# Gate weights stored by 64 tokens in two halves, and 16 gathered rows moved to the last stage

## The chip, the core and the metric

The kernel runs on one core of one Trainium2 chip. The time is device microseconds from start to end of one execution; lower is better. The kernel before takes 2756.99 us, the median of three runs (2752.73 to 2758.27 us). Engines are named as the profile names them: PE is the matrix engine (TensorE) and PEld its weight loads, DVE is VectorE, ACT is ScalarE, POOL is GpSimd, SP is SyncE, which issues most of the DMAs.

## The reference

One transformer-like layer on 1024 tokens of width 1024. A norm and a projection feed a differential attention and a gated linear recurrence; both go through an output projection into the residual. Then comes the part that fills most of the time: for each token, 8 heads pick 16 of 16384 experts (two searches among 128 keys, then the best 16 of their sums), each expert is a single neuron with a row of `expert_down` and a row of `expert_up`, and the chosen 128 rows are weighted, summed and added to the residual. A last norm gives the output.

```python
def peer_ffn(xn, w_query, sub_keys_1, sub_keys_2, expert_down, expert_up):
    ...
    q = (xt @ w_query).reshape(T, PEER_HEADS, 2, PEER_HALF).astype(jnp.float32)
    s1 = jnp.einsum('thd,kd->thk', q[:, :, 0], sub_keys_1.astype(jnp.float32))
    s2 = jnp.einsum('thd,kd->thk', q[:, :, 1], sub_keys_2.astype(jnp.float32))
    v1, i1 = lax.top_k(s1, PEER_TOPK)
    v2, i2 = lax.top_k(s2, PEER_TOPK)
    cand = (v1[..., :, None] + v2[..., None, :]).reshape(T, PEER_HEADS, PEER_TOPK * PEER_TOPK)
    sc, ci = lax.top_k(cand, PEER_TOPK)
    eid = (jnp.take_along_axis(i1, ci // PEER_TOPK, axis=-1) * PEER_N_KEYS
           + jnp.take_along_axis(i2, ci % PEER_TOPK, axis=-1))
    g = jax.nn.softmax(sc, axis=-1)
    ...
        u = expert_down[eb]
        act = jax.nn.gelu(jnp.einsum('thkd,td->thk', u, xb).astype(jnp.float32))
        w = (gb * act).astype(xb.dtype)
        return jnp.einsum('thk,thkd->td', w, expert_up[eb])

def reference(x, ...):
    ...
        n = rmsnorm(h, norm1_g[l])
        p = n @ w_in[l]
        ...
        attn_out = diff_attention(q, k, v, lam, subln_g[l], lambda_init)
        lru_out = rglru_branch(xr, gate, ...)
        h = h + jnp.concatenate([attn_out, lru_out], axis=-1) @ w_out[l]
        h = h + peer_ffn(rmsnorm(h, norm2_g[l]), ...)
    return rmsnorm(h, norm_f_g)
```

## The kernel before

The 1024 tokens are eight blocks of 128. Three blocks (384 tokens, `NG`) do the expert part by *gathering*: for each of a block's 128 slots, POOL issues an indirect DMA that fetches one row of 1024 floats for each of the 128 tokens (line 879, 512 KB), and DVE uses it in one SCALAR_TENSOR_TENSOR, a dot product with the token for `expert_down` (line 896) or a scaled addition into `accg` for `expert_up` (line 906). That is 768 *gathered rows* in all, through five row buffers. Both kinds of DVE instruction are kept in program order.

The other five blocks (640 tokens, `TD`) do the expert part densely over all 16384 experts. An expert tile is the 128 experts that share the first key; there are 128 tiles. For each tile a *down* (`down_all`, 48 matmuls of 320 columns) gives `ga`, the activations of 128 experts by 640 tokens; its weights come by SP as `draw` (512 KB) and are split into a high part `dh` (ACT, line 126) and a low part `dl` (DVE, line 127), two pairs a down. The activations are multiplied by the *gate weights* (zero wherever an expert was not chosen, `ga<-ga,gw`), split into `w_h` and `w_l`, and 30 matmuls a tile (15 for each half of the columns, tile `pu`) add the products with `expert_up` (`uraw`, split into `uh` and `ul`).

The gate weights are made beforehand, in the *one-hot stage*: for 16 tokens at a time (`TB`, here a *block of 16*; there are 40), DVE builds one-hot rows `o` (line 1136) and weighted ones `o1v` (line 1140), ACT builds `o1a` (line 1147, 16 instructions), and 48 matmuls (line 1160) give for each token a 128 by 128 square of weights in PSUM tiles `pg` of four tokens. ACT copies each into a staging tile `st` (line 1163), laid out as [128 experts, 128 keys, `TG` tokens]. When a staging tile has its 32 tokens, two DMAs on ACT's queue (lines 1165 and 1166) store it to `gw_d`, the first 32 keys apart from the other 96. In the last stage SP loads the gate weights of four tiles at a time (`gw`, line 1198, 1280 KB), in runs of 4 keys by 32 tokens, 512 bytes.

Downs can run early: 70 of the 128 are done ahead of the last stage, during the queries, the top-k and above all beside the one-hots, so that PE has work there; their results are kept (`act`, written by ACT's queue). So in the one-hot stage PE alternates between 48 matmuls of a down and 48 of a block of 16.

Gathered rows are spread over the program by counts: `gather_steps(n)` puts n of them behind a piece of other work. `G_ATT`, `G_OUT`, `G_QRY`, `G_TOPK` and `G_OH` say how many fall into the second attention, the second output projection, the second queries, the top-k and the one-hots, and `G_UP` is what remains for the last stage, 466 of the 768. These counts are the program's order. The order on each engine is then made by a scheduler, which plays the program through with estimated times, and lets an instruction pass others on its engine where these are not ready; so where a gathered row stands on DVE is not given by the counts alone.

## Time and profile before

| | |
|---|---|
| median of three runs | 2756.99 us |
| the profiled execution | 2756.29 us, of which its span (first to last instruction) 2754.5 us |
| PE busy | 2626.9 us (95%) |
| DVE busy | 2276.4 us (83%) |
| ACT busy | 1200.6 us (44%) |
| HBM read and written | 690.77 MB and 102.11 MB |

The stages by time from the span's start: the projections and the two attentions to 568 us; the second output projection to about 660 us; the queries and the top-k, with the first early downs, to about 1020 us; the one-hots with early downs to 1408 us; the last stage to 2739 us; the final norms to the end. A busy PE can be short of its peak, since the ends of its matmuls are modelled; the starts of matmuls that follow each other tell its pace.

### The profile page before, as it was taken

The page shows a single profiled execution, that of the slowest core. Times are in us where ns is not written, and L with a number is a line of the kernel's source. Part 1 is how long each engine was busy: PE and PEld are TensorE (multiplying, and loading weights), DVE is VectorE, ACT ScalarE, POOL GpSimd, SP SyncE. Part 2 cuts the span into 40 slices and gives each one's busy share as a digit, 9 for nine tenths or more (in the row PEclk, how much of TensorE's full clock was granted, in tenths as well). Part 3 has the DMA queues.
Part 4 walks back from the last instruction along what each step waited for, and adds up shares of the span by engine and source line. Part 5 has one row for each costly group of instructions (what it writes and reads, how often), then busy time and mean ns, then how long its engine had stood idle before and what let it go on. Part 6 is the DMA issues. An engine that isn't in the chain of part 4 may idle for free.

```text
span 2754.5 us, 43406 instructions
## 1 busy us (share of the span) xinstructions
PE 2626.9 (95%) x15577; PEld 2323.2 (84%) x15577; DVE 2276.4 (83%) x4737; ACT 1200.6 (44%) x2551; POOL 1042.8 (38%) x850
## 2 busy tenths in 40 slices
PE   7989987889999899999999999999999999999996
PEld 6767965747999899999988888888888888888885
DVE  6565878877999978989967789888888888888897
ACT  5763436722324667888853223222223222222222
POOL 1000223353322015443323445444454545545563
PEclk9999988989999999999999999999999999999998
DMA  5446888877675249999999999999999999999986
GB/s 193 154 138 230 314 242 238 259 256 271 233 255 174 92 162 350 356 341 335 338 370 326 334 351 326 336 332 352 339 332 336 330 340 326 348 338 338 338 288 242
DMA packets 319273, 795.75 MB, mean 289 GB/s; under 512 B 26209, under 2 KB 126577, under 8 KB 316497
## 3 DMA queue, kind: packets, MB, share of 16 engines
q0 software_dynamic: 118128, 428.28, 44.2%
q1 hardware_dynamic: 184112, 297.97, 32.1%
q10 hardware_dynamic: 16816, 66.72, 6.0%
q8 instruction: 122, 2.00, 0.3%
q14 instruction: 95, 0.77, 0.1%
HBM read 690.77 MB, written 102.11 MB: 288 GB/s over the span
## 4 chain that ended last, share of the span: by engine, by line
PE 70%; issue 11%; DMA 9%; DVE 6%; POOL 2%; ACT 2%; SPq 0%; DVEq 0%; ACTq 0%; POOLq 0%
PE pu L158 9%; PE pu L161 9%; PE pu L162 9%; PE pd L162 8%; PE pd L158 8%; PE pd L161 8%; PE pg L1160 4%; PE pa L158 3%; PE pa L162 2%; PE pa L161 2%; POOL row L879 2%; DMA row<-in_expert_up,eid 2%; DMA row<-in_expert_down,eid 2%; DVE row L896 1%; PE pa L606 1%
## 5 line engine op out<-in xcount | busy, mean ns | idle before, releaser
L879 POOL DMA_INDIRECT row<-in_expert_up,eid x384 | 513.1, 1336 | 666.9 <-DVE accg L906 542.2
L879 POOL DMA_INDIRECT row<-in_expert_down,eid x384 | 487.9, 1271 | 631.0 <-DVE row L896 504.2
L158 PE MATMUL pd<-xdH,dh 128*128 128x320 f32 x2048 | 639.6, 313 | 6.0 <-ACT dh L126 3.8
L162 PE MATMUL pd<-xdH,dl 128*128 128x320 f32 x2048 | 631.3, 311 | 10.8 <-DVE dl L127 10.8
L161 PE MATMUL pd<-xdL,dh 128*128 128x320 f32 x2048 | 634.6, 310 | 0.0
L906 DVE SCALAR_TENSOR_TENSOR accg<-row,wg,accg 128x1024 f32<-128x1024 f32 x384 | 491.3, 1279 | 27.0 <-DMA row<-in_expert_up,eid 24.1
L161 PE MATMUL pu<-ul,w_h 128*128 128x512 f32 x1280 | 503.5, 393 | 2.5 <-DVE ul L127 2.5
L162 PE MATMUL pu<-uh,w_l 128*128 128x512 f32 x1280 | 499.6, 392 | 0.0
L896 DVE SCALAR_TENSOR_TENSOR row<-row,x2g 128x1024 f32<-128x1024 f32 x384 | 460.6, 1218 | 32.3 <-DMA row<-in_expert_down,eid 29.9
L162 PEld LDWEIGHTS pd<-xdH,dl 128*128 128x128 f32 x2048 | 385.4, 189 | 19.4 <-DVE dl L127 12.8
L158 PE MATMUL pu<-uh,w_h 128*128 128x512 f32 x1280 | 393.5, 394 | 8.3 <-DVE acc L1261 3.3
L158 PEld LDWEIGHTS pd<-xdH,dh 128*128 128x128 f32 x2048 | 387.0, 189 | 14.5 <-ACT dh L126 4.1
L161 PEld LDWEIGHTS pd<-xdL,dh 128*128 128x128 f32 x2048 | 386.8, 189 | 8.2
L126 ACT CAST uh<-uraw 128x512 fp32r<-128x512 f32 x256 | 157.9, 620 | 498.3 <-PE pu L162 397.5
L161 PEld LDWEIGHTS pu<-ul,w_h 128*128 128x128 f32 x1280 | 241.9, 189 | 50.3 <-DVE ul L127 3.7
L158 PEld LDWEIGHTS pu<-uh,w_h 128*128 128x128 f32 x1280 | 238.1, 189 | 52.5 <-issue 3.7
L162 PEld LDWEIGHTS pu<-uh,w_l 128*128 128x128 f32 x1280 | 241.3, 189 | 47.8
L126 ACT CAST dh<-draw 128x512 fp32r<-128x512 f32 x256 | 157.9, 618 | 241.5 <-PE pd L161 226.9
L127 DVE TENSOR_TENSOR ul<-uraw,uh 128x512 fp32r<-128x512 f32 x256 | 175.5, 687 | 77.6 <-ACT uh L126 76.7
L127 DVE TENSOR_TENSOR dl<-draw,dh 128x512 fp32r<-128x512 f32 x256 | 175.4, 687 | 67.3 <-ACT dh L126 65.2
L126 ACT CAST w_h<-ga 128x640 fp32r<-128x640 f32 x128 | 93.3, 729 | 243.1 <-PE pu L161 166.3
L1147 ACT ACTIVATE o1a<-o,slot_a 128x128 bf16<-128x128 bf16 x640 | 194.1, 428 | 1.8 <-DVE o L1136 1.8
(282 smaller groups left out, 4050.7 us busy)
## 6 DMA issues: line engine op xcount, KB each, us to landing
draw<-in_down_t SPq DMA_DIRECT2D x128, 512.0 KB, 7.0
uraw<-in_up_h SPq DMA_DIRECT2D x128, 512.0 KB, 7.2
gw<-gw_d SPq DMA_DIRECT2D x32, 1280.0 KB, 15.2
gw_d<-st ACTq DMA_DIRECT2D x20, 1536.0 KB, 10.4
act<-ga ACTq DMA_DIRECT2D x70, 320.0 KB, 4.9
ga<-act SPq DMA_DIRECT2D x70, 320.0 KB, 9.7
w_d<-w POOLq DMA_DIRECT2D x32, 512.0 KB, 5.1
w<-w_d SPq DMA_DIRECT2D x32, 512.0 KB, 5.5
```

The source lines that it names most:

```text
L126: A.copy(hi, src)
L127: (eng or V).tensor_sub(lo, src, hi.bitcast(F32))
L158: t = T.matmul(ps, wh, mh, start=first, stop=False)
L161: T.matmul(ps, wh, ml, start=False, stop=False)
L162: T.matmul(ps, wl, mh, start=False, stop=last)
L606: T.matmul(pss[:, t - t0, :], qt[:, t * P:(t + 1) * P], kt[:, ct % 2, :], start=True, stop=True)
L879: nc.gpsimd.indirect_dma_start(out=r, out_offset=None, in_=table, in_offset=bass.IndirectOffsetOnAxis(ap=eids[tb][:, s:s + 1], axis=0))
L896: tc.keep_in_program_order(V.scalar_tensor_tensor(r, r, 1.0, x2, op0=ALU.mult, op1=ALU.mult, accum_out=act[:, s:s + 1]))
L906: tc.keep_in_program_order(V.scalar_tensor_tensor(acc, r, w[:, s:s + 1], acc, op0=ALU.mult, op1=ALU.add))
L1147: A.activation(oa[:, g, :, j], o[:, g, 1, :, j], AF.Copy, scale=slot_a[b][:, tt + t:tt + t + 1])
L1160: T.matmul(ps[:, t - t4, :], o[:, g, 0, :, j], part[:, g, :, j], start=i == 0, stop=i == 2)
```

## The change

Staging tiles hold 64 tokens in place of 32, and each is two tiles of 64 keys. So the copy out of PSUM becomes two copies of half the size (160 instructions become 320), 64 tokens are stored by three DMAs of 1, 1 and 2 MB in place of four of 0.5 and 1.5 MB, and a load of gate weights reads runs of 4 keys by 64 tokens, 1024 bytes, the same 1280 KB. There are three buffers of a half tile (16 KB a partition each) where there were two of a whole one of 32 tokens (16 KB). The one-hot tile `o21` gets two buffers in place of three. `G_OUT` goes from 24 to 8, and with it `G_UP` from 466 to 482.

```diff
--- before.py
+++ after.py
@@ -44,11 +44,11 @@
 EG = 8
 EQ = 4
 EARLY = 4
-TG = 32
+TG = 64
 TB = 16
 TI = 2
 
-G_ATT, G_OUT, G_QRY, G_TOPK, G_OH = 64, 24, 46, 0, 168
+G_ATT, G_OUT, G_QRY, G_TOPK, G_OH = 64, 8, 46, 0, 168
 G_UP = 2 * NG * SLOTS - (G_ATT + G_OUT + G_QRY + G_TOPK + G_OH)
 B_OUT, B_CHAIN, B_TURN, B_QRY, B_TOPK = 0, 3, 8, 8, 12
 A_STEPS, A_AHEAD, A_FILL, LRU_AT, WO_AT = 3, 4, 0.5, 0.7, 50
@@ -1113,7 +1113,7 @@
         v12_stack.close()
         tk_stack.close()
         oh = ph.enter_context(tc.tile_pool(name="oh", bufs=2))
-        st_pool = ph.enter_context(tc.tile_pool(name="stage", bufs=2))
+        st_pool = ph.enter_context(tc.tile_pool(name="stage", bufs=3))
         ps_g = ph.enter_context(tc.tile_pool(name="ps_g0", bufs=3, space=PSUM))
         key_f = oh.tile([P, P], F32, name="key_f", bufs=1)
         G.iota(key_f, pattern=[[1, P]], base=0, channel_multiplier=0,
@@ -1132,7 +1132,7 @@
                 return t[:, g0:g0 + GB, :, None, :].broadcast_to([P, GB, n, P, TI]).rearrange(
                     "p g n k i -> p (g n) k i")
 
-            o = oh.tile([P, GB, 2, P, TI], BF, name="o21", bufs=3)
+            o = oh.tile([P, GB, 2, P, TI], BF, name="o21", bufs=2)
             V.tensor_tensor(o.rearrange("p g n k i -> p (g n) k i"),
                             key_t[:, None, :, :].broadcast_to([P, GB * 2, P, TI]),
                             per_slot(slot_k[b], 2), op=ALU.is_equal)
@@ -1150,7 +1150,7 @@
 
         def weights(t0, o, parts):
             if t0 % TG == 0:
-                sts[t0 // TG] = st_pool.tile([P, NK, TG], F32, name="st")
+                sts[t0 // TG] = [st_pool.tile([P, NK // 2, TG], F32, name="st") for _ in range(2)]
             st = sts[t0 // TG]
             for t4 in range(0, TB, 4):
                 ps = ps_g.tile([P, 4, P], F32, name="pg")
@@ -1160,10 +1160,14 @@
                         T.matmul(ps[:, t - t4, :], o[:, g, 0, :, j], part[:, g, :, j],
                                  start=i == 0, stop=i == 2)
                 c = t0 % TG + t4
-                A.copy(st[:, :, c:c + 4], ps.rearrange("p t i -> p i t"))
+                for half in range(2):
+                    A.copy(st[half][:, :, c:c + 4],
+                           ps[:, :, half * NK // 2:(half + 1) * NK // 2].rearrange("p t i -> p i t"))
             if (t0 + TB) % TG == 0:
-                nc.scalar.dma_start(gw_d[0][t0 // TG], st[:, :E_FIRST, :])
-                nc.scalar.dma_start(gw_d[1][t0 // TG], st[:, E_FIRST:, :])
+                n = NK // 2 - E_FIRST
+                nc.scalar.dma_start(gw_d[0][t0 // TG], st[0][:, :E_FIRST, :])
+                nc.scalar.dma_start(gw_d[1][t0 // TG][:, :n, :], st[0][:, E_FIRST:, :])
+                nc.scalar.dma_start(gw_d[1][t0 // TG][:, n:, :], st[1])
 
         sts = {}
         last_five, last = last, None
```

The scheduler's order changes in more places than the diff. Counted on DVE, the gathered rows (lines 896 and 906) stand like this:

| stage, by DVE's own instructions | before | after |
|---|---|---|
| up to the second output projection | 61 | 61 |
| second output projection (lines 1000 to 1004) | 27 | 11 |
| from there to the first one-hot | 46 | 46 |
| first to last one-hot | 112 | 156 |
| from there to the first `ul` | 8 | 9 |
| last stage | 514 | 485 |

In the steady part of the one-hot stage, from the 60th to the 136th `dl` on DVE (38 downs), there stand 107 gathered rows (32 of line 896, 75 of line 906), 36 `o` and 35 `o1v` before, and 149 (53 and 96), 37 and 37 after. In the same stretch PE has 36 and 37 blocks of 16.

DVE in the middle of the one-hot stage before, two blocks of 16 (`o_13866` and `o_14024` are their one-hot tiles):

```order
L1136 TENSOR_TENSOR o_13866<-key_t,slot_k_8430 128x4096
L906 SCALAR_TENSOR_TENSOR accg<-row,wg,accg 128x1024
L127 TENSOR_TENSOR dl<-draw,dh 128x512 x2
L1140 TENSOR_TENSOR o1v<-o_13866,slot_w_8435 128x4096
L1136 TENSOR_TENSOR o_14024<-key_t,slot_k_8431 128x4096
L906 SCALAR_TENSOR_TENSOR accg<-row,wg,accg 128x1024 x2
L127 TENSOR_TENSOR dl<-draw,dh 128x512
L906 SCALAR_TENSOR_TENSOR accg<-row,wg,accg 128x1024
L127 TENSOR_TENSOR dl<-draw,dh 128x512
L906 SCALAR_TENSOR_TENSOR accg<-row,wg,accg 128x1024
L1140 TENSOR_TENSOR o1v<-o_14024,slot_w_8436 128x4096
```

and at the like place after, one block and the head of the next:

```order
L1136 TENSOR_TENSOR o_13900<-key_t,slot_k_8380 128x4096
L906 SCALAR_TENSOR_TENSOR accg<-row,wg,accg 128x1024
L1140 TENSOR_TENSOR o1v<-o_13900,slot_w_8385 128x4096
L906 SCALAR_TENSOR_TENSOR accg<-row,wg,accg 128x1024 x2
L127 TENSOR_TENSOR dl<-draw,dh 128x512
L906 SCALAR_TENSOR_TENSOR accg<-row,wg,accg 128x1024
L127 TENSOR_TENSOR dl<-draw,dh 128x512
L906 SCALAR_TENSOR_TENSOR accg<-row,wg,accg 128x1024
L1136 TENSOR_TENSOR o_14061<-key_t,slot_k_8381 128x4096
```

The piece of before has one gathered row in its first block and four in its second; the piece after has five in its one block. `o1v` also stands closer behind its own `o`.

DVE at the program's end, where `ul` is the last work that PE needs from DVE and `acc` takes the last sums from PE; before:

```order
L127 TENSOR_TENSOR ul<-uraw,uh 128x512
L906 SCALAR_TENSOR_TENSOR accg<-row,wg,accg 128x1024
L127 TENSOR_TENSOR ul<-uraw,uh 128x512
L906 SCALAR_TENSOR_TENSOR accg<-row,wg,accg 128x1024
L127 TENSOR_TENSOR ul<-uraw,uh 128x512
L906 SCALAR_TENSOR_TENSOR accg<-row,wg,accg 128x1024
L1261 TENSOR_TENSOR acc_16753<-acc_16753,pu 128x512
L906 SCALAR_TENSOR_TENSOR accg<-row,wg,accg 128x1024 x2
L1261 TENSOR_TENSOR acc_16754<-acc_16754,pu 128x512
L906 SCALAR_TENSOR_TENSOR accg<-row,wg,accg 128x1024
L1261 TENSOR_TENSOR acc_16755<-acc_16755,pu 128x512
```

and after, around the norm of the last gathered block (line 729), which follows its last row:

```order
L127 TENSOR_TENSOR ul<-uraw,uh 128x512
L142 SCALAR_TENSOR_TENSOR n_r<-n_t,n_r 128x1
L141 SCALAR_TENSOR_TENSOR n_t<-n_r,n_v 128x1
L142 SCALAR_TENSOR_TENSOR n_r<-n_t,n_r 128x1
L729 SCALAR_TENSOR_TENSOR row<-accg,n_r,gfb 128x1024
L127 TENSOR_TENSOR ul<-uraw,uh 128x512 x6
L1265 TENSOR_TENSOR acc_16853<-acc_16853,pu 128x512
L1265 TENSOR_TENSOR acc_16854<-acc_16854,pu 128x512
L1265 TENSOR_TENSOR acc_16855<-acc_16855,pu 128x512
L1265 TENSOR_TENSOR acc_16856<-acc_16856,pu 128x512
L1265 TENSOR_TENSOR acc_16857<-acc_16857,pu 128x512
L127 TENSOR_TENSOR ul<-uraw,uh 128x512 x7
```

The gathered rows ran to the last sums; now the last one stands ahead of the last 14 `ul`.

ACT where a staging tile is stored; before:

```order
L1165 DMA gw_d<-st 128x1024
L1166 DMA gw_d<-st 128x3072
L1147 ACTIVATE o1a<-o_12601,slot_a_8439 128x128 x5
L126 CAST dh<-draw 128x512
L1044 ACTIVATE ga<-pd 128x320
L126 CAST dh<-draw 128x512
L1044 ACTIVATE ga<-pd 128x320
L1163 COPY st<-pg 128x128x4
L1069 DMA act_12685<-ga 128x640
L1163 COPY st<-pg 128x128x4 x3
L1147 ACTIVATE o1a<-o_12759,slot_a_8440 128x128 x16
```

and after, where line 1164 is the half copy and the first three after the stores all go into the first half:

```order
L1168 DMA gw_d<-st 128x2048
L1169 DMA gw_d<-st 128x2048
L1170 DMA gw_d<-st 128x4096
L126 CAST dh<-draw 128x512
L1147 ACTIVATE o1a<-o_13576,slot_a_8390 128x128 x16
L1044 ACTIVATE ga<-pd 128x320
L126 CAST dh<-draw 128x512
L1044 ACTIVATE ga<-pd 128x320
L1164 COPY st<-pg 128x64x4 x3
L1069 DMA act_13660<-ga 128x640
L1164 COPY st<-pg 128x64x4 x5
```

Copies into the second half need the buffer that lines 1168 and 1169 have just begun to store; before, the tile that the next copies fill had been stored two blocks of 16 earlier.

## Rows read from the trace of the kernel before

**Rows 1.** The page: busy time, share and instructions of each engine.

```profile
PE 2626.9 (95%) x15577; PEld 2323.2 (84%) x15577; DVE 2276.4 (83%) x4737; ACT 1200.6 (44%) x2551; POOL 1042.8 (38%) x850
```

**Rows 2.** Stages: length, busy of PE, PEld, DVE, ACT, POOL; clock, DMA share, GB/s.

```profile
570.00:660.00 90.00, 86.04 (x291) 46.86 (x290) 72.96 (x146) 20.97 (x39) 46.52 (x37) 0.98 0.89 317
1076.00:1409.00 333.00, 333.00 (x3278) 329.31 (x3277) 300.32 (x261) 293.91 (x803) 140.29 (x95) 1.00 0.93 343
1409.00:1500.00 91.00, 81.97 (x465) 75.59 (x464) 61.48 (x96) 26.75 (x49) 28.86 (x24) 0.96 1.01 362
1500.00:2500.00 1000.00, 1000.00 (x5128) 876.72 (x5126) 839.66 (x1168) 280.72 (x488) 498.12 (x392) 1.00 0.95 335
2700.00:2755.00 55.00, 32.92 (x121) 25.51 (x120) 42.50 (x93) 12.22 (x29) 15.62 (x12) 0.81 0.61 216
```

**Rows 3.** Chain of waits, in order of time: two one-hot blocks.

```profile
1155.69 2.77 PE pg L1160 x48
...
1165.55 2.77 PE pg L1160 x48
```

**Rows 4.** Timeline of VectorE in one block: start, length, work, idle before it.

```profile
1158.43 2.29 DVE L1140 TENSOR_TENSOR o1v<-o,slot_w 128x4096 bf16<-128x4096 bf16 x1 [0.37 <-PE pg L1160]
1160.64 2.28 DVE L1136 TENSOR_TENSOR o<-key_t,slot_k 128x4096 bf16<-128x4096 bf16 x1
...
1163.99 1.22 DVE L896 SCALAR_TENSOR_TENSOR row<-row,x2g 128x1024 f32<-128x1024 f32 x1
...
1165.13 0.68 DVE L127 TENSOR_TENSOR dl<-draw,dh 128x512 fp32r<-128x512 f32 x1
1165.74 1.22 DVE L896 SCALAR_TENSOR_TENSOR row<-row,x2g 128x1024 f32<-128x1024 f32 x1
...
2698.37 2.60 DVE L906 SCALAR_TENSOR_TENSOR accg<-row,wg,accg 128x1024 f32<-128x1024 f32 x2 [1.36 <-DMA row<-in_expert_up,eid]
2700.90 0.69 DVE L127 TENSOR_TENSOR ul<-uraw,uh 128x512 fp32r<-128x512 f32 x1
```

**Rows 5.** DMA queues and issues from 1076 to 1409 us.

```profile
q0 software_dynamic: 13423, 48.87, 43.9%
q10 hardware_dynamic: 9710, 46.63, 34.0%
q1 hardware_dynamic: 5003, 18.22, 14.7%
...
gw_d<-st ACTq DMA_DIRECT2D x18, 1536.0 KB, 10.2
...
row<-in_expert_up,eid POOLq DMA_INDIRECT x63, 8.2
```

**Rows 6.** Timeline of ScalarE in the same block.

```profile
1155.57 0.62 ACT L126 CAST dh<-draw 128x512 fp32r<-128x512 f32 x1 [0.82 <-PE pd L161]
1156.10 0.43 ACT L1044 ACTIVATE ga<-pd 128x320 f32<-128x320 f32 x1
1156.43 0.58 ACT L1163 COPY st<-pg 128x512 f32<-128x512 f32 x1
...
1158.97 0.45 ACT L1147 ACTIVATE o1a<-o,slot_a 128x128 bf16<-128x128 bf16 x1
```

**Rows 7.** DMA queue of SP from 1500 to 2600 us, and one wait.

```profile
q1 hardware_dynamic: 104042, 142.00, 37.3%
...
DVE ga L1209 <- DMA gw<-gw_d: 5.2, 1, 5.2
```

**Rows 8.** The end: TensorE, then VectorE.

```profile
2703.52 0.76 PE L158 MATMUL pu<-uh,w_h 128*128 128x512 f32 x1 [3.31 <-DVE acc L1261]
...
2722.21 0.49 PE L158 MATMUL pu<-uh,w_h 128*128 128x512 f32 x1 [1.88 <-ACT uh L126]
...
2724.74 0.80 PE L161 MATMUL pu<-ul,w_h 128*128 128x512 f32 x1 [0.84 <-DVE ul L127]
...
2734.38 2.60 DVE L906 SCALAR_TENSOR_TENSOR accg<-row,wg,accg 128x1024 f32<-128x1024 f32 x2
```

## The prediction

> **What bounds the kernel now.** I read the page's busy times first: PE 95%, DVE 83%, ACT 44% [rows 1]. Then the stages: from 1076 to 1409 us (one-hots) PE is busy for 333.00 of 333 us and from 1500 to 2500 us (last stage) for all 1000, while the DMA engines are busy for 93% and 95% [rows 2]. So PE sets both stages, and DMA has little left in either. In the one-hot stage the chain of waits shows PE's pace: a block of 16 starts 9.86 us after the one before, 2.77 us of `pg` and 7.09 us of a down [rows 3]. PE is idle elsewhere: 4 us of the 90 around the second output projection, 9 of 91 where the last stage begins, 22 of the last 55 [rows 2]. Those are all that a change of this kind can win; all else is matmuls that stay.
>
> **Copies.** 160 copies of 512 columns become 320 of 256. Four copies take from 1156.43 to 1158.97 us, 2.54 us, about PE's 2.77 us for the four squares; 320 columns of `ga` take 0.33 us from start to start [rows 6]. Two halves at 0.33 us make 0.66 us in place of 0.64 us, so next to nothing; at 0.43 us, the full length of `ga`, they make 0.86 us, 0.9 us a block. ACT has 0.82 us idle in a block [rows 6], which hides either but for 0.1 us. I take nothing; without that cover it would be at most 0.9 us times 40, 36 us.
>
> **Two buffers for the one-hot tile.** `o` now waits for the matmuls for which only `o1v` waited, 0.37 us in the block shown [rows 4]. An `o` costs 2.2 us, which DVE could lose per block if it were early; below it is late, so I take nothing (0 to 8 us).
>
> **Gathered rows on DVE in the one-hot stage.** This is the term that decides. The order puts 149 rows where 107 stood, over the same 38 downs. DVE's prices from start to start: `o1v` 2.21 us, `o` the same length and so 2.2 us, a row of line 896 1.14 us, a `dl` 0.61 us, and of line 906 1.265 us (two from 2698.37 to 2700.90) [rows 4]. Before: 71 one-hots at 2.2 make 156.6 us, 76 `dl` 46.4 us, 32 and 75 rows 131.4 us, together 334 us beside PE's 38 times 7.09 plus 36 times 2.77, 369 us: 91%, and the trace has 90% [rows 2]. After: 163.2 plus 46.4 plus 53 and 96 rows at 181.8, 391 us, beside 372 us of PE. DVE works in order and every down waits for its `dl`, so the stage cannot be shorter than DVE's work: 19 us more, whatever else happens. That is the low end.
>
> **The same rows on DMA.** Over the 333 us, POOL's queue moved 48.87 MB in 43.9%, 334 GB/s, 1.57 us for a row of 0.524 MB; ACT's 46.63 MB in 34.0%, 412 GB/s, 2.55 us for a block's weights (1.05 MB) and 0.80 us for an `act`; SP's 18.22 MB in 14.7%, 372 GB/s, 1.41 us for a `draw` [rows 5]. Before: 107 rows 168 us, 38 downs 84 us, 36 blocks 92 us, 344 of 369 us: 93%, just the share in the trace [rows 2], so the prices hold. After: 234 plus 84 plus 94, 412 us in PE's 372: 40 us more with no engine ever idle. A row arrives 8.2 us after its issue [rows 5] and there are five buffers, so DVE, waiting in order for a row, holds back `dl` and with it PE. POOL, which issues them, is busy for 140 of the 333 us [rows 2], 195 by the new count, and binds nothing. I take 42 us, the DMA sum and a little for waits that do not overlap; the ends are 19 (DVE alone) and 75 us (next part).
>
> The highest share of DMA in these stages is 1.01, at 362 GB/s [rows 2]. The Trainium skill (DMA: Bandwidth & Descriptors, Where 436 GB/s comes from) says that for traffic with HBM the HBM side binds, at about 358 GB/s a core. The trace about agrees, 343 GB/s at 93% being 369 at 100%. By the page the stretch's 149 MB would take 417 us, an estimate, and the sum below would be 5 us higher.
>
> **Staging.** After a store, the fourth copy of the next block needs a buffer with 2 MB just issued. A store of 1.5 MB lands after 10.2 us [rows 5]; the next block's copies begin 9.86 less 2.54, 7.3 us, after the last ones [rows 3, 6], and the fourth comes some 1.5 us later. So ACT waits over 1 us at nine boundaries, 11 us, and at a landing half as long again, 15 us, six, 54 us. With PE already late by DMA's pace, most is covered; uncovered, it takes the stage to 75 us.
>
> **The gate weight loads.** 1 KB runs in place of 512 bytes. From 1500 to 2600 us SP's queue moved 142.00 MB in 37.3% of 1100 us, 410 us [rows 7]. With 28 loads of 1.31 MB, 36.7 MB, and the rest at the 372 GB/s of [rows 5], the loads take 127 us, and at that rate 99: 28 us of DMA time saved. PE never waits there, and DVE waited for `gw` once, 5.2 us [rows 7]. I count nothing in the middle of the stage. At its beginning, 3 of the 9 idle us may go (between 9 saved and 5 lost, since 2 MB more of stores, 5 us at 412 GB/s, go ahead of the first load).
>
> The Trainium skill (Perfetto Trace Analysis, DMA Optimizations) calls larger transfers the first remedy where DMA binds, and transfers under 2 KB costly. Queue rates agree, 346 against 372 GB/s; but by [rows 2] PE binds here, so by the trace its 28 us buy nothing, and by the rule alone the sum would be 28 us lower.
>
> **Output projection.** 16 rows fewer: of 4 us of idle PE I take 3 (0 to 6, with a clock below full after the idle).
>
> **The end.** Before, rows stand between the last `ul` and `acc`, and PE waits 3.31, 1.88 and 0.84 us there [rows 8]; the granted clock, full elsewhere, is 0.81 over the last 55 us, which on 33 busy us costs up to 6 us [rows 2]. After, no row stands behind the last 14 `ul`. I take 6 us of waits, 4 of slow clock, and 4 for two additions and a norm ahead of the last `acc` [rows 8]: 14 us saved (4 to 20). The 29 rows fewer in the last stage win nothing else, PE being full.
>
> **Sum.** 42 less 14, 3 and 3 is 22 us more. The profiled execution took 2756.3 us, 0.7 below the median; so 2778.3 beside it and 2779 us as a median.
>
> **Rivals.**
> - *DVE alone decides.* The DMA engines move the rows 5% faster than at my prices and only DVE's 19 us appear: 19 less 20 is -1, 2756 us. For it: a share over 1.00 [rows 2]. Against it: prices that give 93% exactly. 15%.
> - *The stage keeps its pace (faster).* DVE and DMA work off the rows in what looked like idle time before and behind the stretch, and PE never waits; only the savings remain, 20 us: 2737 us. It decides if blocks still follow at 9.86 us. Against it: DVE cannot run further ahead than two buffers of `dl` and `o`, a few us. 10%.
> - *Staging stalls come on top.* ACT waits for its buffer at every boundary, `dh` and the copies behind it wait too, and PE, having idled, runs at half clock for a while: 30 us over the forecast, 2809 us. It decides if landings pass 13 us. 20%.
> - My forecast: 55%.
>
> **Range and chances.** 2750 to 2812 us: it holds the first and third rival, leaves out the second and little above. Within 0.2% (5.5 us) is what a measurement cannot tell from no change. Faster by more: the second rival and a little of the first, 0.11. Within: most of the first and the lower edge of the forecast, 0.13. Slower: 0.76.
>
> **What would show it.** In the profile after, blocks of 16 should follow at 10.6 to 11.5 us, with DMA near full and PE waiting for `dl`; 9.86 us there proves me wrong. `st` waiting for a store by several us at each boundary is the third rival. The end should have no `accg` in its last 40 us and PE at full clock. The last stage's middle should keep PE full. If its PE were idle, a bound I have not priced is there.

## The result, and the profile after

The changed kernel takes 2852.27 us (median of four runs, 2849.6 to 2861.15) beside 2757.63 us for the kernel before in the same series: a ratio of 1.0353, with a 95% interval of 1.0331 to 1.0376. It is slower by 95 us, where 22 were forecast and the range ended at 2812 us. The direction came out right, though not by the mechanism that was forecast. More than half of the miss in size lies in the one-hot stage (96 us longer, 42 forecast), the rest mostly where the last stage begins and at its end.

Stage by stage, from the starts of the first and last instructions of each kind on TensorE in the two profiled executions (of `pu`, those of line 162). The one of after is the run of 2861.15 us, the slowest of its four, so the stages add up to 105 us and not to 95. Here and below a stage's length is that of one execution; executions of one kernel lie 7 to 19 us apart in all, so a few us of a stage decide nothing.

| stage | before, us | after, us | measured | forecast |
|---|---|---|---|---|
| up to the first matmul of the second output projection | 568.1 | 574.1 | +6.0 | 0 |
| output projection and queries | 277.9 | 274.9 | -3.0 | -3 |
| one-hots (last query matmul to last `pg`) | 561.4 | 657.5 | +96.1 | +42 |
| entry (last `pg` to first `pu`) | 44.1 | 56.8 | +12.7 | -3 |
| last stage (first to last `pu`) | 1287.3 | 1285.1 | -2.2 | -14 with the end |
| end | 15.7 | 11.0 | -4.7 | |
| span | 2754.5 | 2859.4 | +104.9 | +22 |

The 6 us of the first row arise before anything that the change touches; among all kernels here, that start varies from 561.2 to 574.1 us.

The page's first line, and the stages as in [rows 2] (columns as there; the stretches are put where the same work now runs):

```profile
PE 2651.0 (93%) x15577; PEld 2343.5 (82%) x15577; DVE 2283.1 (80%) x4737; ACT 1203.1 (42%) x2711; POOL 1088.3 (38%) x850
```

```profile
574.00:664.00 90.00, 87.41 (x301) 47.21 (x300) 57.70 (x132) 21.85 (x43) 26.84 (x22) 0.99 0.67 233
1076.00:1409.00 333.00, 283.29 (x2590) 277.86 (x2589) 282.86 (x250) 237.07 (x757) 192.59 (x108) 0.94 0.87 317
1500.00:1597.00 97.00, 73.90 (x485) 68.85 (x484) 51.12 (x81) 27.83 (x63) 27.44 (x23) 0.89 0.88 327
1597.00:2597.00 1000.00, 993.98 (x5077) 868.82 (x5076) 833.66 (x1151) 277.38 (x483) 500.67 (x388) 1.00 0.92 333
2804.00:2859.00 55.00, 44.77 (x198) 36.75 (x196) 26.69 (x72) 14.18 (x32) 0.00 (x0) 0.94 0.27 95
```

The second line is the one to look at. In the 333 us where PE was never idle before, it is idle for 49.7 us, its clock is granted at 0.94, and yet every other engine, and DMA too (0.87, where [rows 2] had 0.93), does less than is possible. No resource is full. That is the sign of a closed loop: engines that wait for each other in a circle. Of the waits of that stretch, these (engine and instruction, what it waited for, us in total, times, longest):

```profile
PE pg L1160 <- ACT st L1164: 49.7, 21, 7.8
ACT o1a L1147 <- DVE o L1136: 33.6, 17, 6.9
ACT st L1164 <- DMA gw_d<-st: 22.3, 6, 5.8
DVE o L1136 <- PE pg L1160: 19.2, 11, 5.1
DVE accg L906 <- DMA row<-in_expert_up,eid: 14.4, 9, 3.4
DVE row L896 <- DMA row<-in_expert_down,eid: 9.3, 4, 4.2
```

PE's whole idle time is one wait: for the copy `st` that frees a PSUM buffer of `pg`. ACT, which makes the copies, waits for `o`; DVE, which makes `o`, waits for PE. Two DMA waits feed into the circle: the store of the half tile, and late rows. Blocks of 16 no longer follow at 9.86 us [rows 3] but come in groups of four, by the starts of `o` from 1260.0 us on: 17.0, 10.9, 11.7 and 10.5 us. The long one stands behind each chunk of 64 tokens. Its timeline, first DVE, then ACT:

```profile
1260.00 2.28 DVE L1136 TENSOR_TENSOR o<-key_t,slot_k 128x4096 bf16<-128x4096 bf16 x1
...
1266.21 1.28 DVE L906 SCALAR_TENSOR_TENSOR accg<-row,wg,accg 128x1024 f32<-128x1024 f32 x1
1269.35 1.28 DVE L906 SCALAR_TENSOR_TENSOR accg<-row,wg,accg 128x1024 f32<-128x1024 f32 x1 [1.86 <-DMA row<-in_expert_up,eid]
1270.55 0.68 DVE L127 TENSOR_TENSOR dl<-draw,dh 128x512 fp32r<-128x512 f32 x1
1274.67 1.28 DVE L906 SCALAR_TENSOR_TENSOR accg<-row,wg,accg 128x1024 f32<-128x1024 f32 x1 [3.44 <-DMA row<-in_expert_up,eid]
1276.95 2.29 DVE L1136 TENSOR_TENSOR o<-key_t,slot_k 128x4096 bf16<-128x4096 bf16 x1 [0.99 <-PE pg L1160]
```

```profile
1258.99 0.33 ACTq L1168 DMA_DIRECT2D gw_d<-st  x1
...
1262.50 4.84 ACT L1147 ACTIVATE o1a<-o,slot_a 128x128 bf16<-128x128 bf16 x16
...
1268.62 0.64 ACT L1164 COPY st<-pg 128x256 f32<-128x256 f32 x2
1275.05 0.92 ACT L1164 COPY st<-pg 128x256 f32<-128x256 f32 x3 [5.80 <-DMA gw_d<-st]
1276.95 0.65 ACT L1164 COPY st<-pg 128x256 f32<-128x256 f32 x2 [0.97 <-PE pg L1160]
```

At 1259 us 4 MB of stores are issued at once. ACT's fourth copy gets its half tile at 1275.05 us, 16 us later; the second late row reaches DVE at 1274.67 us. Two waits of different origin end 0.4 us apart, so either of them hides the other; keep that for the experiments.

That a long block stands behind each store holds over the whole stage. By the starts of `o` from 1020.7 to 1493.7 us, the nine blocks that begin behind a store take 16.3 us in the mean and the 28 others 11.7 us.

The DMA queues and issues, as in [rows 5], from 1076 to 1409 us:

```profile
q0 software_dynamic: 15566, 56.68, 49.8%
q10 hardware_dynamic: 6503, 34.15, 25.0%
...
gw_d<-st ACTq DMA_DIRECT2D x13, 1024.0 KB, 11.0
gw_d<-st ACTq DMA_DIRECT2D x6, 2048.0 KB, 19.5
...
row<-in_expert_up,eid POOLq DMA_INDIRECT x76, 7.9
```

Rows are 56.68 MB in place of 48.87, all else is less because the stage runs slower, and a row's median time to landing has not grown (7.9 against 8.2 us). A median hides the few rows behind a store, which are the ones that count.

### The profile page after: what moved, and what is told of

Same layout as the page of the kernel before. It is cut to its first block, busy times and chain, and to the rows that moved or that the text cites. A ratio compares the mean times of both kernels' runs of the same rounds, so it can differ in the third digit from the quotient of the medians.

```text
span 2859.4 us, 43548 instructions
## 1 busy us (share of the span) xinstructions
PE 2651.0 (93%) x15577; PEld 2343.5 (82%) x15577; DVE 2283.1 (80%) x4737; ACT 1203.1 (42%) x2711; POOL 1088.3 (38%) x850
## 4 chain that ended last, share of the span: by engine, by line
PE 61%; issue 14%; DMA 11%; DVE 7%; ACT 4%; POOL 4%; SPq 0%; ACTq 0%; POOLq 0%; DVEq 0%
PE pu L161 10%; PE pu L158 10%; PE pu L162 9%; PE pd L158 6%; PE pd L162 6%; PE pd L161 6%; POOL row L879 3%; DMA row<-in_expert_down,eid 3%; PE pa L998 2%; DMA gw_d<-st 2%; PE pa L158 2%; PE pa L162 2%; PE pa L161 2%; ACT o1a L1147 1%; DVE row L896 1%
## 5 line engine op out<-in xcount | busy, mean ns | idle before, releaser
L879 POOL DMA_INDIRECT row<-in_expert_up,eid x384 | 553.3, 1441 | 549.3 <-DVE accg L906 407.6
L158 PE MATMUL pd<-xdH,dh 128*128 128x320 f32 x2048 | 646.6, 316 | 1.9 <-ACT dh L126 1.5
L158 PEld LDWEIGHTS pd<-xdH,dh 128*128 128x128 f32 x2048 | 393.6, 192 | 11.0 <-ACT dh L126 2.7
L161 PEld LDWEIGHTS pd<-xdL,dh 128*128 128x128 f32 x2048 | 392.9, 192 | 7.2
L161 PEld LDWEIGHTS pu<-ul,w_h 128*128 128x128 f32 x1280 | 241.4, 189 | 49.7 <-DVE ul L127 2.6
## 6 DMA issues: line engine op xcount, KB each, us to landing
gw_d<-st ACTq DMA_DIRECT2D x20, 1024.0 KB, 11.4
gw_d<-st ACTq DMA_DIRECT2D x10, 2048.0 KB, 19.5
```

The source lines that it names most:

```text
L158: t = T.matmul(ps, wh, mh, start=first, stop=False)
L161: T.matmul(ps, wh, ml, start=False, stop=False)
L879: nc.gpsimd.indirect_dma_start(out=r, out_offset=None, in_=table, in_offset=bass.IndirectOffsetOnAxis(ap=eids[tb][:, s:s + 1], axis=0))
```

## The experiments

Theories at the outset. **Rows**: the additional gathered rows set the stage, through DVE or DMA (the prediction's own term). **Two buffers**: two `o` buffers in place of three tie DVE, ACT and PE into a loop. **Staging**: ACT waits for a half tile that is still being stored. Later a fourth came, the **burst**: 4 MB at once make rows late. All runs in one table; rows are the gathered rows that stand among the 60th to 136th `dl`, in the order of the instructions on DVE. Four kernels ran once and have no interval.

| kernel | rows | one-hots, us | entry | end | time, us | ratio to before, interval |
|---|---|---|---|---|---|---|
| before | 107 | 561.4 | 44.1 | 15.7 | 2757.6 | 1 |
| changed | 149 | 657.5 | 56.8 | 11.0 | 2852.3 | 1.0353 (1.0331 to 1.0376) |
| o_two | 140 | 600.4 | 49.1 | 10.9 | 2789.0 | single run |
| o_two_thin | 105 | 596.9 | 35.7 | 37.2 | 2813.8 | single run |
| no_wait_o_three | 134 | 578.6 | 33.3 | 11.0 | 2840.8 | single run |
| no_wait | 164 | 609.5 | 27.9 | 11.0 | 2863.0 | single run |
| stores_of_half_two | 148 | 653.9 | 54.7 | 11.0 | 2844.5 | 1.0325 (1.0304 to 1.0346) |
| stores_of_quarter_three | 117 | 576.6 | 50.6 | 16.9 | 2777.1 | 1.0071 (1.0050 to 1.0093) |
| changed_thin | 109 | 609.7 | 46.3 | 60.6 | 2848.6 | 1.0346 (1.0321 to 1.0371) |
| gather_eight | 107 | 562.7 | 47.8 | 36.5 | 2774.1 | 1.0059 (1.0036 to 1.0083) |
| stores_spread | 150 | 646.4 | 45.5 | 10.9 | 2830.8 | 1.0276 (1.0258 to 1.0295) |
| o_two_split | 140 | 594.3 | 48.8 | 10.8 | 2784.5 | 1.0124 (1.0103 to 1.0145) |
| o_two_four_squares | 105 | 560.9 | 36.5 | 37.2 | 2775.3 | 1.0087 (1.0068 to 1.0106) |
| queries_eight_more | 107 | 567.8 | 48.0 | 10.9 | 2755.4 | 1.0012 (1.0002 to 1.0022) |
| one_burst | 132 | 648.1 | 45.5 | 17.0 | 2845.0 | 1.0337 (1.0315 to 1.0358) |
| four_stores | 132 | 636.7 | 43.9 | 16.9 | 2837.0 | 1.0299 (1.0282 to 1.0316) |
| changed_four_squares | 129 | 602.5 | 49.4 | 11.0 | 2796.0 | 1.0154 (1.0133 to 1.0174) |
| o_two_four_rows | 118 | 553.5 | 51.2 | 10.8 | 2754.7 | 1.0005 (0.9992 to 1.0017) |
| changed_four_squares_thin | 118 | 592.1 | 50.7 | 42.4 | 2810.1 | 1.0194 (1.0167 to 1.0221) |

**Two `o` buffers alone (o_two, o_two_thin).** Kernel before with this line; o_two_thin also has G_OH 108 in place of 168, so fewer rows there.

```diff
-            o = oh.tile([P, GB, 2, P, TI], BF, name="o21", bufs=3)
+            o = oh.tile([P, GB, 2, P, TI], BF, name="o21", bufs=2)
```

> The kernel before with one edit of the change: two buffers for the one-hot tile in place of three. Its order has 140 gathered rows in the 38 downs of the steady one-hot stage (107 before, 149 after). From the last query matmul to the last one-hot matmul the kernel before takes 561.5 us and the changed one 657.5. Rows theory (each row over 107 costs 96/42 = 2.3 us): 33 rows, 75 us, some 2815 us in all with the end 15 us shorter. Buffer theory (the loop from the one-hot matmuls over o, o1a and the copies sets the pace, whatever the rows): 60 to 96 us, 2800 to 2840 us. Staging theory (the wait for the store of a half tile is all): nothing, 2745 us.

> The same with G_OH 108 in place of 168 (the other 60 rows in the last stage): 105 rows in the 38 downs, two fewer than before. Rows theory: the stage takes its 561 us, in all 2757 us and some 15 us for 19 rows behind the last ul. Buffer theory: 60 to 96 us longer in the stage, 2830 to 2870 us. Staging theory: as the rows theory.

One line of the kernel before costs 36 us with two rows fewer than before, and 39 with 33 more. So the buffer costs this, and not the number of rows; both are single runs, but o_two_split and o_two_four_squares below bear them out. A block of o_two_thin and the head of the next show the loop, first on DVE, then on ACT:

```profile
1257.03 2.29 DVE L1136 TENSOR_TENSOR o<-key_t,slot_k 128x4096 bf16<-128x4096 bf16 x1
...
1265.14 1.29 DVE L127 TENSOR_TENSOR dl<-draw,dh 128x512 fp32r<-128x512 f32 x2
1266.35 1.28 DVE L906 SCALAR_TENSOR_TENSOR accg<-row,wg,accg 128x1024 f32<-128x1024 f32 x1
1267.54 2.28 DVE L1136 TENSOR_TENSOR o<-key_t,slot_k 128x4096 bf16<-128x4096 bf16 x1
```

```profile
1259.35 4.84 ACT L1147 ACTIVATE o1a<-o,slot_a 128x128 bf16<-128x128 bf16 x16 [1.83 <-DVE o L1136]
1264.06 0.61 ACT L126 CAST dh<-draw 128x512 fp32r<-128x512 f32 x1
...
1264.90 0.60 ACT L126 CAST dh<-draw 128x512 fp32r<-128x512 f32 x1
...
1265.73 0.56 ACT L1163 COPY st<-pg 128x512 f32<-128x512 f32 x1
```

```profile
1266.35 0.28 PE L1160 MATMUL pg<-o1v,o 128*128 128x128 bf16 x2 [0.27 <-ACT st L1163]
```

`o` begins at 1257.03 and `o1a`, which waits for it, at 1259.35 us. The sixteen `o1a` hold ACT for 4.7 us; behind them, in order, stand both `dh` (until 1265.4) and the copies. One branch goes on over DVE: `dl` needs `dh`, a row stands behind it, then the next `o`. The other goes over PE: the copy at 1265.73 frees a PSUM buffer, at 1266.35 us (the line of PE) the 12 matmuls of the last tile `pg` start, and only their end frees an `o` buffer. Either way the circle takes 10.3 to 10.5 us, longer than PE's 9.86. In the kernel before, from 1076 to 1409 us, ACT has one wait of any size, for PE to free a `dh`, and none for `o`:

```profile
ACT dh L126 <- PE pd L161: 28.1, 34, 1.2
```

**The stores without the wait, first try (no_wait_o_three, no_wait).** Changed kernel; the stores read another tile (`xH`, here through its view `xf`) in the same sizes, so what is stored are not the gate weights (the other two stores likewise). The first also has three `o` buffers and two of the half tile.

```diff
-                nc.scalar.dma_start(gw_d[0][t0 // TG], st[0][:, :E_FIRST, :])
+                nc.scalar.dma_start(gw_d[0][t0 // TG], xf[:, :E_FIRST, :])
```

> The changed kernel with three one-hot buffers, two staging buffers, and stores of the same size that read a finished tile in place of the staging tile, so that no copy ever waits for a store; the gate weights that it stores are not the computed ones. 134 rows in the 38 downs. Rows theory: 27 rows, 62 us, some 2800 us. Buffer theory and staging theory: the stage takes its 561 us, and with the shorter end 2735 to 2745 us.

> The changed kernel with stores of the same size that read a finished tile, so that no copy waits for a store (the gate weights stored are not the computed ones); two one-hot buffers and three staging buffers as changed. 164 rows in the 38 downs. Rows theory: 57 rows, 130 us, 2870 us. Buffer theory: 60 to 96 us, 2810 to 2850 us. Staging theory: 2740 us.

These two single runs tell little. The stores, which then depended on nothing, were put by the scheduler into the query stage: output projection and queries took 358 us in place of 275, and the one-hot stage had 42 MB less to move. In the next runs the stores read a tile that the block does fill, and so stay in place.

**The wait for the half tile (stores_of_half_two, stores_of_quarter_three).** Changed kernel:

```diff
-                nc.scalar.dma_start(gw_d[0][t0 // TG], st[0][:, :E_FIRST, :])
-                nc.scalar.dma_start(gw_d[1][t0 // TG][:, :n, :], st[0][:, E_FIRST:, :])
+                nc.scalar.dma_start(gw_d[0][t0 // TG], st[1][:, :E_FIRST, :])
+                nc.scalar.dma_start(gw_d[1][t0 // TG][:, :n, :], st[1][:, E_FIRST:, :])
```

For the second: `o21` three buffers, tiles of 96 keys (one buffer) and 32 keys (two), four stores of the latter.

> The changed kernel, but its three stores of a chunk of 64 tokens all read the second half tile, so that the same 4 MB go to the same places at the same time while a half tile that is to be filled next has never been read by a store that is still under way (the stored values of the first 64 keys are not the computed ones). Two o buffers and 148 gathered rows stay. Theory (two causes side by side: two o buffers cost about 39 us of the one-hot stage, the wait for a half tile's store the other 57): the stage takes 600 to 610 us in place of 657, ACT no longer waits on gw_d<-st, the whole run takes about 2800 us (2790 to 2815). Rival (rows and DMA traffic set the stage, as the prediction had it): both are unchanged, so the run stays at 2840 to 2855 us. Rival (the o buffers alone): also unchanged, 2840 to 2855 us.

> As the run before, with three o buffers. To make room, the first 96 keys are staged in one buffer and the last 32 in two, and all four 1 MB stores of a chunk read the last (the stored values of the first 96 keys are not the computed ones; the copies are of 384 and 128 columns). 117 gathered rows stand among the downs of the stage in place of 149. Theory (buffers and staging wait): both causes are gone, the one-hot stage takes 560 to 575 us and the run 2750 to 2775 us. Rival (only the rows): 117 in place of 107 rows at 2.3 us each are 23 us, so about 2780 us. Rival (DMA traffic with stores of 64 tokens, whatever the buffers): 2800 us or more.

The theory missed by 50 us in the first: without any wait for a store the stage takes 653.9 us, 3.6 less. The late rows were right behind. From 1076 to 1409 us the changed kernel's two waits for rows were 14.4 and 9.3 us (above); here they are longer:

```profile
PE pg L1160 <- ACT st L1164: 37.5, 23, 4.8
DVE accg L906 <- DMA row<-in_expert_up,eid: 18.5, 15, 2.7
DVE row L896 <- DMA row<-in_expert_down,eid: 13.4, 4, 4.9
```

In the second, with three `o` buffers, the stage falls to 576.6 us and the time to that of gather_eight below, which has the same `G_OUT`. It gets back 81 of the 96 us, though 4 MB are still stored at once. This run alters buffers, rows (117) and stores together, so it does not show which of them brings it. The changed kernel with three `o` buffers and its own stores was not run.

**Rows alone (changed_thin, gather_eight).** The first is the changed kernel with fewer rows in the stage:

```diff
-G_ATT, G_OUT, G_QRY, G_TOPK, G_OH = 64, 8, 46, 0, 168
+G_ATT, G_OUT, G_QRY, G_TOPK, G_OH = 64, 8, 46, 0, 112
```

The second is the kernel before with the change's move of 16 rows alone:

```diff
-G_ATT, G_OUT, G_QRY, G_TOPK, G_OH = 64, 24, 46, 0, 168
+G_ATT, G_OUT, G_QRY, G_TOPK, G_OH = 64, 8, 46, 0, 168
```

> The changed kernel with G_OH 112 in place of 168: 109 gathered rows among the downs of the one-hot stage in place of 149, about the 107 of before; two o buffers and the staging wait stay, and 33 rows stand behind the last ul, which costs the end some 20 to 25 us as in o_two_thin. Theory (buffers and staging wait): the one-hot stage stays within 15 us of the changed kernel's 657 us, the run takes 2855 to 2885 us. Rival (rows on DVE and DMA, the prediction's term): the stage falls by 40 rows at 2.3 us, 90 us, to about 565 us, and the run takes 2780 to 2790 us.

> The kernel before with G_OUT 8 in place of 24 and nothing else: 107 rows among the downs of the one-hot stage as before, 19 rows behind the last ul in place of 6. Theory: the second output projection takes 3 us less, the end 13 rows at up to 1.27 us, 10 to 16 us, more, so 2764 to 2772 us. Rival (the move is what brings rows into the one-hot stage and costs time there): the one-hot stage takes over 580 us and the run over 2775 us. Rival (rows are absorbed by idle DVE time in the last stage): 2752 to 2757 us.

changed_thin contradicts both: 609.7 us is neither within 15 us of 657 nor near 565. So rows do matter in the changed kernel (40 rows, 48 us), and they do not in o_two (35 rows, 3.5 us). What differs is the staging by 64 tokens, which with few rows adds 13 us to o_two_thin. The starts of `o` say where the rows come in: o_two's 37 blocks from 1015.7 to 1432.4 us take 11.3 us in the mean, so against o_two, 45 of the changed kernel's 57 us more stand in its nine blocks behind a store (16.3 us). In changed_thin the like nine take 11.9 us and the others 11.3. gather_eight shows that the moved rows do no harm in the stage; behind the last `ul`, 19 rows in place of 6 make the end 21 us longer.

**Burst or copies (stores_spread, o_two_split).** The first stores a chunk as four times 1 MB, one behind each block, from the second half tile, with the copies kept in program order and G_OH 154. The second is o_two with each copy in two halves.

```diff
+            for _ in range(len(late) if t0 + TB == TD else 1 if late else 0):
+                tc.keep_in_program_order(nc.scalar.dma_start(*late.pop(0)))
```

```diff
-                A.copy(st[:, :, c:c + 4], ps.rearrange("p t i -> p i t"))
+                for k in (0, NK // 2):
+                    A.copy(st[:, k:k + NK // 2, c:c + 4],
+                           ps[:, :, k:k + NK // 2].rearrange("p t i -> p i t"))
```

> As stores_of_half_two (two o buffers, no store that a half tile waits for, the stored values of the first 64 keys not the computed ones), but the 4 MB of a chunk go out as four stores of 1 MB, one behind each block of 16, in place of 4 MB at once behind the fourth; G_OH 154 keeps 150 gathered rows among the downs (148 there). Theory (the burst: 4 MB at once make the gathered rows late, DVE waits for them in order, and with two o buffers each such wait goes round the loop of DVE, ACT and PE): the long block behind each chunk, 13 to 17 us, goes, DVE waits on rows for under 20 us in place of 44, the one-hot stage takes 600 to 620 us in place of 654, the run 2785 to 2810 us. Rival (150 rows are simply too many for DVE in a loop with two o buffers): the stage stays at 645 to 660 us, the run at 2835 to 2855. Rival (the copies in two halves): the same as the second.

> o_two (the kernel before with two o buffers, 140 rows, TG 32) with each copy out of PSUM made in two halves of 64 keys, as the change makes them, and nothing else. Theory (burst of stores): nothing to speak of, the four more copies of a block lie in ACT's loop for 0.1 to 0.2 us, so the one-hot stage takes 600 to 610 us (600 in o_two) and the run 2788 to 2800 us. Rival (the copies in two halves make the difference between o_two and stores_of_half_two): about 650 us, and the run 2835 us.

Copies in halves cost nothing, as the prediction had it. stores_spread missed: the long block behind each chunk is gone (11.6 and 11.8 us in turn), but every block now takes as long as the other three of a group took (11.7 us in the middle), or longer. Keeping the copies in order had moved rows too: four or five stand in each block, two of them between the `dl` and the next `o`. So the comparison was made again with the same order on DVE but for a few instructions.

**The burst again (one_burst, four_stores).** Both with G_OH 136 and the copies kept in order; they differ only in how a chunk's 4 MB are stored.

> stores_of_half_two (the changed kernel, all stores of a chunk read the second half tile, so the stored values of the first 64 keys are not the computed ones and no half tile waits for a store) with G_OH 136 and the copies kept in order: 132 gathered rows, four to a block, two o buffers, a chunk's 4 MB stored at once. Theory (burst): one block in four is 2 to 6 us longer than its neighbours, with DVE waiting for a row from DMA in it, and the one-hot stage takes 15 to 50 us more than that of four_stores. Rival (rows and DVE's own work in the loop): both take the same within 8 us, and no block in four stands out.

> one_burst, with a chunk's 4 MB stored as four times 1 MB, one behind each block of 16; the order on DVE is the same row for row. Theory (burst): blocks follow evenly at 10.5 to 11.6 us, DVE waits for rows for under 15 us in the stage, and the stage takes 605 to 630 us. Rival (rows and DVE's own work): as one_burst within 8 us.

The burst costs 11.4 us of the stage in the two profiled executions and 8 us between the medians, less than expected; four_stores also stays above the 605 to 630 us of its theory. In four_stores DVE never waits for a row from 1076 to 1409 us; in one_burst:

```profile
DVE accg L906 <- DMA row<-in_expert_up,eid: 9.2, 6, 2.8
DVE row L896 <- DMA row<-in_expert_down,eid: 7.4, 2, 4.9
```

But four_stores still takes 637 us with eight rows fewer than o_two, which takes 600. A block of it on DVE suggests why:

```profile
1276.20 2.28 DVE L1136 TENSOR_TENSOR o<-key_t,slot_k 128x4096 bf16<-128x4096 bf16 x1
...
1284.70 0.69 DVE L127 TENSOR_TENSOR dl<-draw,dh 128x512 fp32r<-128x512 f32 x1 [0.15 <-PE pg L1160]
1285.31 2.60 DVE L906 SCALAR_TENSOR_TENSOR accg<-row,wg,accg 128x1024 f32<-128x1024 f32 x2
1287.83 2.28 DVE L1136 TENSOR_TENSOR o<-key_t,slot_k 128x4096 bf16<-128x4096 bf16 x1
```

The block takes 11.63 us: 2.3 to `o1a`, 6.2 to the second `dl`, 0.6, and two rows of 1.26. Its other two rows, between `o` and `dl`, are free: DVE still waits 0.78 us before the first `dl` and 0.15 us before the second. o_two_thin's block above, with one row behind its second `dl`, takes 10.51 us. So a row in the loop costs some 1.2 us a block, a row beside it nothing; the count of rows says little.

This is not what sets the changed kernel apart from o_two. Counted over the blocks that begin from 1040 to 1440 us, 2.3 rows a block stand behind the last `dl` in four_stores and 2.2 in one_burst, 0.8 in the changed kernel and 0.7 in o_two. The order that costs four_stores its 37 us over o_two came with keeping the copies in order, so what a burst costs in the changed kernel's own order was not measured by itself.

**Opening the loop (o_two_four_squares, changed_four_squares, o_two_four_rows, changed_four_squares_thin).** A fourth PSUM buffer for `pg`, its room taken from the transposes of the top-k: the last tile `pg` then waits for no copy of its own block. With it the scheduler, which no longer sees `o` late, also places `dl` and rows otherwise, so this opens both branches at once.

```diff
-        ps_t = ph.enter_context(tc.tile_pool(name="ps_k", bufs=2, space=PSUM))
+        ps_t = ph.enter_context(tc.tile_pool(name="ps_k", bufs=1, space=PSUM))
...
-        ps_g = ph.enter_context(tc.tile_pool(name="ps_g0", bufs=3, space=PSUM))
+        ps_g = ph.enter_context(tc.tile_pool(name="ps_g0", bufs=4, space=PSUM))
```

Made in o_two_thin, in the changed kernel, in o_two, and in the changed kernel with G_OH 121.

> o_two_thin (the kernel before with two o buffers and G_OH 108, 105 rows) with four PSUM buffers for the squares pg in place of three (one in place of two for the transposes of the top-k make room). Theory (the loop: o waits for the last square's matmuls, these for a copy st that frees a PSUM buffer, that stands on ACT behind o1a and two downs, and o1a waits for o): a fourth buffer takes the copy out of the loop; blocks follow at 9.9 to 10.0 us in place of 10.3, PE's waits on st go, and the one-hot stage takes 561 to 580 us in place of 597; the rows behind the last ul cost 20 us or so at the end as before, so the run takes 2780 to 2795 us (2814 without). Rival (o waits for all 48 matmuls in any case, and DVE's own order sets the loop): 590 us or more, and the run stays at 2805 to 2815 us.

> The changed kernel with four PSUM buffers for the squares pg in place of three (one in place of two for the transposes of the top-k), nothing else by hand; 129 rows stand among the downs in place of 149. Theory (all of the 96 us pass through the loop of o, o1a, st and pg, and late rows cost only because a block has no slack in it): the one-hot stage takes 565 to 590 us in place of 657, PE's waits on st fall from 67 to under 20 us, and the run takes 2755 to 2785 us. Rival (the loop costs 36 us and the burst the rest by itself): 610 to 625 us, the run 2805 to 2820.

> The kernel before with two o buffers and four PSUM buffers for the squares, G_OH left at 168: 118 rows among the downs of the one-hots, none behind the last ul. Theory (with the loop open two o buffers cost nothing, and the end without rows is a gain of 5 us): the one-hot stage takes 558 to 575 us, the end 11 us, the run 2745 to 2757 us. Rival (rows are what costs): 11 rows more at 2.3 us, 25 us more in the stage, the run 2775 us or more.

> changed_four_squares with G_OH 121: 118 gathered rows among the downs, as in o_two_four_rows, so that the two differ by the staging of 64 tokens in halves (and by 22 rows behind the last ul, from G_OUT 8, some 25 us at the end). Theory (a burst of 4 MB makes rows late and DVE waits for them whatever their number): the one-hot stage takes 580 to 600 us (547 in o_two_four_rows, 602 with 129 rows), DVE waits for rows for over 20 us, the run takes 2800 to 2815 us. Rival (129 rows were too many, staging costs nothing with the loop open): 547 to 565 us, the run 2765 to 2782 us.

o_two_four_squares is the cleanest run of the study: 560.9 us against 596.9, and 561.4 before. All of the 36 us are back with two `o` buffers in place, so the loop, of which the PSUM buffers are a part, is their cause. The kernel before was not run with a fourth buffer; since its PE was never idle from 1076 to 1409 us [rows 2], there was little for it to gain in that stretch. ACT's wait for `o`, which was 52.3 us in o_two_thin from 1076 to 1409 us, is now

```profile
ACT o1a L1147 <- DVE o L1136: 7.8, 8, 1.7
```

In the changed kernel the same edit gives back 55 us of the 96, less than the theory had (565 to 590). PE's wait for `st` is gone there (1.5 us), and what is left is rows:

```profile
PE pd L162 <- DVE dl L127: 15.5, 10, 4.9
DVE accg L906 <- DMA row<-in_expert_up,eid: 19.3, 13, 2.7
DVE row L896 <- DMA row<-in_expert_down,eid: 18.8, 6, 5.3
```

DVE waits 38 us for rows, holds back `dl`, and PE waits for that. With 118 rows the stage takes 592.1 us where o_two_four_rows, with as many and staging by 32 tokens, takes 553.5 (the expectation's 547 us end with an earlier `pg`, the last of `o1v`): with the loop open, the staging by 64 tokens still costs 39 us between these two.

**A version without the loss (queries_eight_more).** The kernel before with `G_QRY` 54 in place of 46, to have the end without rows.

> The kernel before with G_QRY 54 in place of 46: eight gathered rows go from the last stage to the queries, none stands behind the last ul (6 before), and 107 stand among the downs of the one-hots as before. Theory (the change's one gain, an end without rows, can be had without its two o buffers and its longer staging): the end takes 11 us in place of 16, the queries hide the rows, so 2749 to 2753 us. Rival (rows in the queries cost what they save): 2753 to 2758 us. Rival (DMA or DVE in the queries is late and the early downs with it): over 2758 us.

The end is 4.8 us shorter as expected, the one-hot stage 6 us longer, the ratio 1.0012 (1.0002 to 1.0022), within its first rival. It is no gain, and neither is o_two_four_rows (its shorter one-hot stage comes back as a longer entry). No version here beats the kernel before.

## Why the prediction was wrong

- **The step that failed** is "Two buffers for the one-hot tile", which took nothing (0 to 8 us): it measured 36 us, by o_two_thin against before, and o_two_four_squares gives 36 back. The prediction asked only whether DVE loses time when `o` waits. The engine that pays is ACT, whose `o1a` waits for `o` and which works in order, with every `dh` and every copy behind; and PE pays through both. [Rows 6] showed ACT with 0.82 us to spare in a block of 9.86.
- **Rows on DMA**, the term that was to decide, was a sum of transfers. It forecast a full DMA at 10.6 to 11.5 us a block; the four blocks above took 12.5 in the mean, at a DMA share of 0.87. That its prices gave 93% was no test of them: they were worked out from the busy shares that add up to 93%. o_two, with 140 rows, moved 351 GB/s in that stretch and lost 3.5 us to its 35 rows. Throughput over the stage was not the limit; single rows late behind a burst of stores were what DVE waited for. That the change came out slower, as forecast, is therefore partly luck. The Trainium skill (DMA: Bandwidth & Descriptors, Where 436 GB/s comes from) gives some 358 GB/s as the ceiling of traffic with HBM; the 317 GB/s of the changed kernel at a share of 0.87 would be 364 at 1, about that, and the stage did not reach it. It is not a strict ceiling in these traces: from 1506 to 1556 us, behind the last stores, the changed kernel moved 403 GB/s.
- **Rows on DVE**: the bound of 19 us is not broken and does not bind, with DVE busy for 282.86 of 333 us.
- **Staging** was priced at 11 to 54 us and then taken as covered by PE's lateness. The third rival named the stalls: ACT waits 33.5 us for stores, nine times from 1030 us on, and PE runs on behind such a wait at a granted clock of 0.50 (last section). Its mechanism is there; its price, 30 us over the forecast, is not shown for the wait alone, which gives back 3.6 us of the stage when it is taken away by itself, for the late rows end with it. Both together stand in the nine blocks behind a store, 42 us longer than nine of the others.
- **Copies** in halves cost nothing (o_two_split, 594.3 against 600.4 us). Right. **Output projection**: -3.0, right in size (gather_eight, where that edit stands alone, has -2.2).
- **Entry**: 3 us saved were forecast, 12.7 lost. PE is idle for 17.6 us there, 6.1 before. The longest wait is for a `dl` behind two rows that are late after the last 4 MB of stores, issued at 1507 us; the other stands before the first `pu`, where the trace names no releaser, but the times fit a chain from the gate weights' first load over `ga` and `w_h`:

```profile
1518.67 1.23 DVE L896 SCALAR_TENSOR_TENSOR row<-row,x2g 128x1024 f32<-128x1024 f32 x1 [4.58 <-DMA row<-in_expert_down,eid]
1524.82 1.22 DVE L896 SCALAR_TENSOR_TENSOR row<-row,x2g 128x1024 f32<-128x1024 f32 x1 [4.91 <-DMA row<-in_expert_down,eid]
1526.71 0.63 PE L162 MATMUL pd<-xdH,dl 128*128 128x320 f32 x1 [8.78 <-DVE dl L127]
...
1557.88 0.82 DVE L1213 TENSOR_TENSOR ga<-ga,gw 128x640 f32<-128x640 f32 x1 [7.33 <-DMA gw<-gw_d]
1559.57 0.77 PE L158 MATMUL pu<-uh,w_h 128*128 128x512 f32 x1 [7.21 <-issue]
```

gather_eight and o_two, which stage 32 tokens, have the second wait too (7.4 and 6.8 us) but not the first, so the late rows are what the change adds here; this is read from the traces and not tried by itself. The one wait for `gw` that the prediction took from [rows 7] ends at 1444.54 us, so it too belongs to the entry and not to the stretch from 1500 to 2600 us.
- **The end**: 14 us forecast, 4.7 measured at the end and 2.2 in the last stage. The rows are gone from it and the clock is 0.94 in place of 0.81, as forecast; but 1000 us of the last stage have 6 us of idle PE, which they had not before, in four waits for `ul`, `uh` and `dl` of up to 1.9 us.

Adding up the one-hot term in the order of the runs: 36 us for two buffers (before to o_two_thin), 13 for staging by 64 tokens with few rows (to changed_thin), 48 for 40 more rows on top of both (to the changed kernel). The last 48 are not divided by a run. By the blocks' starts they stand mostly behind the stores, where late rows and the half tile's wait hide each other; the burst alone is 11 in one_burst against four_stores, in another order on DVE. The parts also add up otherwise in another order: the loop opened last gives 55.

## What to carry to other kernels

Before a buffer is taken from a tile, follow its release through every engine that works in order: what the waiting engine has queued behind, who waits for that, and whether the path comes back to the tile. If it does, its length is a floor for the block, and an instruction costs by whether it stands in that path, not by the engine's busy share. Where two waits end together, removing either shows little; vary them together, or open the loop that both pass through.

## What the runs showed of the hardware

- A burst of stores on one queue delays transfers on another. With 4 MB issued at once (1, 1 and 2 MB), the 2 MB store landed after 19.5 us in the median and rows behind it kept DVE waiting for up to 4.2 us a time, though the median row landed as fast as before; in one_burst, with 4 MB at once, DVE waited 16.6 us for rows in the 333 us compared, and in four_stores, with the same 4 MB in steps of 1 MB, not at all. stores_spread, also in steps, has one such wait, of 5.3 us, whose cause is open.
- After a wait at a boundary PE ran at the lower of its two clocks. In the chain of waits of the changed kernel, behind a store of the half tile and 5.75 us of idle PE, matmuls of a down follow at 0.27 us where 0.147 us (7.09 us for 48) is the pace before [rows 3], for some 17 matmuls. The granted clock from 1324.4 to 1330.3 us is 0.50 (1.2 of 2.4 GHz), and 1.00 behind that. From 1076 to 1409 us, 75 matmuls of downs follow at that pace, none in the kernel before, which makes some 9 us by the difference of 0.12 us:

```profile
1310.31 13.59 DMA gw_d<-st
...
1326.21 0.27 PE pd L161
1326.48 0.27 PE pd L162
```
